# A softmax over a vocabulary: VectorE's and ScalarE's programs as loops, with six pieces a tile for five

## Chip, cores and metric

One core of a Trainium2 chip. The metric is the device time of one execution in microseconds (us). Before the change, three runs gave 2490.64, 2491.82 and 2493.5 us, median 2491.82.

## The reference

```python
batch, seq, vocab = 16, 256, 32768          # logits, float32; temperature 1.0
scaled = logits / temperature
scaled = scaled - scaled.max(axis=-1, keepdims=True)
exp_scaled = np.exp(scaled)
return exp_scaled / exp_scaled.sum(axis=-1, keepdims=True)
```

It is a softmax of 4096 rows of 32768 floats: 537 MB are read and 537 MB written.

## The kernel before, in words

A row is cut into two halves of 16384 floats, which lie on neighbouring partitions. So there are 8192 half rows, and 64 tiles of 128 partitions x 16384 floats (8 MB each). Three places in the on-chip memory (`xs`) hold one tile each; tile g stands in place g mod 3 and is computed in place.

Within a tile the work goes by five pieces of 4096, 4096, 4096, 2560 and 1536 columns (L11):

- VectorE takes each piece's maximum, negated (L146). ScalarE then takes the exponential with this maximum as bias, in place, and adds the piece up as it goes (L159). Every piece so has its own maximum and its own sum.
- When the last exponential is done, VectorE swaps maxima and sums with the neighbouring partition (a stream shuffle, L173), takes the least negated maximum of the row (L177), ScalarE turns the differences into ten correction factors (`ee`, L184), VectorE multiplies and adds (L190), inverts (L202) and makes one factor a piece (L209).
- Then the pieces are scaled in place: two of them on ScalarE (L216, those of `_ON_ACT`, 4096 and 2560 columns), three on VectorE (L219).

All this is written out for 64 tiles, one after the other: the program of each engine is straight, with one running semaphore for each engine (`Stream`, L17) and two sets of small tiles (`t`, `ee`, `junk`, `row`) used in turn. VectorE's own order is maxima, totals, scalings of one tile, and then the maxima of the next; it does not start a tile before the one before it is scaled.

SP issues all transfers on one queue, in an order written out by hand (`transfers`, L63). In the middle of the run it is: load of tile i, as soon as tile i-3 has been stored; store of tile i-1, as soon as it is scaled; and so on. A load is issued at L242, a store at L265. The ends differ: tile 0 comes as a load of 15360 columns and sixteen narrow ones of 8 rows x 1024 columns (L253), tile 3 and the store of tile 0 come in halves, and the store of the last tile, 63, goes in four quarters of 4096 columns, each when its own columns are scaled. `loads` and `stores` (`Lanes`, L44) are semaphores that count sixteen for each transfer, one mark from each of the sixteen DMA engines.

Of the kernel before, what the change touches and what calls it, by code (L numbers as in the profile page):

```python
# [8 lines left out]
_W = 16384  # L9
_BUFS = 3  # L10
_PIECES = (4096, 4096, 4096, 2560, 1536)  # L11
_ON_ACT = (2, 3)
_LAST_STORE = 4096
_NARROW = 1024


class Stream:  # L17


    def __init__(self, nc, engine, name):  # L20
        self.engine = engine
        self.sem = nc.alloc_semaphore(name)
        self.count = 0
        self.seen = {}

    def wait(self, *tokens):
        need = {}
        for sem, value in tokens:
            key = id(sem)
            if value > max(self.seen.get(key, 0), need.get(key, (None, 0))[1]):  # L30
                need[key] = (sem, value)
        for key, (sem, value) in need.items():
            self.engine.wait_ge(sem, value)
            self.seen[key] = value

    def done(self, instruction):
        self.count += 1
        instruction.then_inc(self.sem, 1)
        return (self.sem, self.count)


class Lanes:


    def __init__(self, nc, name):
        self.nc = nc
        self.name = name
        self.sems = {}
        self.counts = {}

    def add(self, key, instruction):
        if key not in self.sems:
            self.sems[key] = self.nc.alloc_semaphore(f"{self.name}_{'_'.join(map(str, key))}")
            self.counts[key] = 0
        self.counts[key] += 16
        instruction.then_inc(self.sems[key], 16)
        return (self.sems[key], self.counts[key])

    def tokens(self):
        return [(self.sems[k], self.counts[k]) for k in self.sems]  # L60


def transfers(n):  # L63
    half = _W // 2
    whole = [(0, _W)]
    halves = [(0, half), (half, half)]
    quarters = [(s, _LAST_STORE) for s in range(0, _W, _LAST_STORE)]
    wide = [(0, _W - _NARROW)]
    plan = [("L", 0, wide), ("N", 0, [(_W - _NARROW, _NARROW)]), ("L", 1, whole), ("L", 2, whole)]
    plan += [("S", 0, halves), ("L", 3, halves), ("S", 1, whole), ("S", 2, whole)]  # L70
    for i in range(4, n - 2):
        plan += [("L", i, whole), ("S", i - 1, whole)]
    plan += [("L", n - 2, whole), ("L", n - 1, whole)]
    plan += [("S", n - 3, whole), ("S", n - 2, whole), ("S", n - 1, quarters)]
    return plan
# [3 lines left out]
def kernel(  # L79
# [20 lines left out]
    K = len(_PIECES)  # L100
    starts = [sum(_PIECES[:k]) for k in range(K)]
    assert sum(_PIECES) == _W
# [4 lines left out]
    T = [nc.alloc_sbuf_tensor(f"t{q}", [P, 4 * K], fp32) for q in range(2)]  # L107
    E = [nc.alloc_sbuf_tensor(f"ee{q}", [P, 2 * K], fp32) for q in range(2)]
    J = [nc.alloc_sbuf_tensor(f"junk{q}", [P, 2 * K], fp32) for q in range(2)]
    R = [nc.alloc_sbuf_tensor(f"row{q}", [P, 4], fp32) for q in range(2)]  # L110

    sp = Stream(nc, nc.sync, "sp")
    dve = Stream(nc, nc.vector, "dve")
    act = Stream(nc, nc.scalar, "act")
    loads = Lanes(nc, "ld")
    stores = Lanes(nc, "st")
    landed = {}
    stored = {}
    scaled = {}
    hist = {}  # L120

    def overlapping(parts, s, n):
        return [token for (a, m), token in parts.items() if a < s + n and s < a + m]

    class Tile:

        def __init__(self, g):
            self.g = g
            self.base = (g % _BUFS) * _W
            self.t, self.e, self.j, self.r = T[g % 2], E[g % 2], J[g % 2], R[g % 2]  # L130
            self.tv = self.t[:, 0 : 4 * K].rearrange("p (a b k) -> p a b k", a=2, b=2)
            self.sums = None
            scaled[g] = {}

        def piece(self, k):
            s = self.base + starts[k]
            return X[:, s : s + _PIECES[k]]

        def exponentials(self, k):
            t = self.t  # L140
            if k == 0 and self.g >= 2:
                dve.wait(*hist[self.g - 2])
            xs = self.piece(k)
            dve.wait(*overlapping(landed[self.g], starts[k], _PIECES[k]))
            m = dve.done(
                nc.vector.tensor_reduce(  # L146
                    out=t[:, k : k + 1], in_=xs, axis=mybir.AxisListType.X, op=A.max, negate=True
                )
            )
            if inv_t != 1.0:  # L150
                dve.wait(m)
                m = dve.done(
                    nc.vector.tensor_scalar_mul(
                        out=t[:, k : k + 1], in0=t[:, k : k + 1], scalar1=inv_t
                    )
                )
            act.wait(m)
            self.sums = act.done(
                nc.scalar.activation(  # L159
                    out=xs,  # L160
                    in_=xs,
                    func=Exp,
                    bias=t[:, k : k + 1],
                    scale=inv_t,
                    accum_out=t[:, K + k : K + k + 1],
                )
            )

        def totals(self):
            t, e, r, tv = self.t, self.e, self.r, self.tv  # L170
            dve.wait(self.sums)
            sh = dve.done(
                nc.vector.stream_shuffle(out=t[:, 2 * K : 4 * K], in_=t[:, 0 : 2 * K], mask=swap)  # L173
            )
            dve.wait(sh)
            mx = dve.done(
                nc.vector.tensor_reduce(  # L177
                    out=r[:, 0:1], in_=tv[:, :, 0, :], axis=mybir.AxisListType.XY, op=A.min
                )
            )  # L180
            act.wait(mx)
            ev = e[:, 0 : 2 * K].rearrange("p (a k) -> p a k", a=2)
            ee = act.done(
                nc.scalar.activation(  # L184
                    out=ev, in_=tv[:, :, 0, :], func=Exp, bias=r[:, 0:1], scale=-1.0
                )
            )
            dve.wait(ee)
            tr = dve.done(
                nc.vector.tensor_tensor_reduce(  # L190
                    out=self.j[:, 0 : 2 * K].rearrange("p (a k) -> p a k", a=2),
                    in0=ev,
                    in1=tv[:, :, 1, :],
                    scale=1.0,
                    scalar=0.0,
                    op0=A.mult,
                    op1=A.add,
                    accum_out=r[:, 1:2],
                )
            )  # L200
            dve.wait(tr)
            rc = dve.done(nc.vector.reciprocal(out=r[:, 2:3], in_=r[:, 1:2]))  # L202
            dve.wait(rc)
            hist[self.g] = (ee, tr)

        def scale(self):
            f = self.j
            w = dve.done(
                nc.vector.tensor_scalar_mul(out=f[:, 0:K], in0=self.e[:, 0:K], scalar1=self.r[:, 2:3])  # L209
            )  # L210
            act.wait(w)
            dve.wait(w)
            for k in range(K):
                xs = self.piece(k)
                if k in _ON_ACT:
                    token = act.done(nc.scalar.mul(out=xs, in_=xs, mul=f[:, k : k + 1]))  # L216
                else:
                    token = dve.done(
                        nc.vector.tensor_scalar_mul(out=xs, in0=xs, scalar1=f[:, k : k + 1])  # L219
                    )  # L220
                scaled[self.g][starts[k], _PIECES[k]] = token
            hist[self.g] += tuple(scaled[self.g].values())

    def compute(g):
        a = Tile(g)
        for k in range(K):
            a.exponentials(k)
        a.totals()
        a.scale()

    plan = transfers(G)
    for (what, g, parts), (what_next, _, _) in zip(plan, plan[1:] + [(None, None, None)]):
        base = (g % _BUFS) * _W
        rows = slice(g * P, (g + 1) * P)
        if what == "L":
            landed[g] = {}
            for k, (s, n) in enumerate(parts):
                if g >= _BUFS:
                    sp.wait(*overlapping(stored[g - _BUFS], s, n))
                landed[g][s, n] = loads.add(  # L240
                    (g % _BUFS, k),
                    nc.sync.dma_start(out=X[:, base + s : base + s + n], in_=x[rows, s : s + n]),  # L242
                )
# [59 lines left out]
```

## Time and profile before

| what | value |
|---|---|
| profiled execution | 2491.0 us |
| span of its trace | 2489.2 us |
| moved by DMA | 1073.89 MB, mean 431 GB/s over the span |
| DMA busy, by slices | 9 tenths or more in 39 of 40 slices, 8 in the last |
| VectorE: maxima (L146), 320 | 1117.3 us busy |
| VectorE: scalings (L219), 192 | 354.9 us busy |
| ScalarE: exponentials (L159), 320 | 965.9 us busy |
| ScalarE: scalings (L216), 128 | 385.9 us busy |
| VectorE waits for loads (L146) | 681.3 us in 60 waits |
| VectorE waits for the last exponential (L173) | 221.4 us in 64 waits |
| load, issue to landing, median | 48.4 us |
| store, issue to landing, median | 29.5 us |

A tile's own chain on the engines, from the start of its first maximum to the end of its last scaling, is about 28 us (tile at 2370.60: last scaling ends at 2398.95). The tiles follow each other at 38.6 us in the middle of the run.

How to read the views: DVE is VectorE, ACT is ScalarE, SP the engine that issues transfers. The busy share of an engine is a mean over the span. A DMA share of 1.00 means that all sixteen DMA engines work; packets are counted where they start, so a short window can show more than 1. The queue called "instruction" carries the engines' own programs from memory. The trace also keeps each DMA packet's start, size and duration, and the moment of each completion mark; where the text speaks of those, they are read from these records. In the tables of windows "x" counts instructions.

### The profile page before, as it was taken

Reading aid. Unit: us, or ns where it says so; the run is one execution under the profiler, and the core shown is the slowest. Engines: PE = TensorE matmul, PEld = TensorE weight load, DVE = VectorE, ACT = ScalarE, POOL = GpSimd, SP = SyncE. Lnnn points to the kernel's source line nnn. Section 1 sums busy time; section 2 is a strip of 40 time slices with the busy share of each in tenths; the row PEclk is TensorE's granted clock in tenths of the full one; section 3 lists DMA queues with packets and bytes.
Section 4 is the critical chain, followed back from the end, with each engine's and each line's share of the span. In section 5 each row is a group of like instructions: output and inputs, shape, how many; then the busy total and the mean of one; then the engine's idle time right before and its main releaser. Section 6 shows DMA issues by size and latency. Waiting matters only on the chain.

```text
span 2489.2 us, 2061 instructions
## 1 busy us (share of the span) xinstructions
DVE 1529.5 (61%) x960; ACT 1390.4 (56%) x833; POOL 0.2 (0%) x4
## 2 busy tenths in 40 slices
DVE  5845665655656556565565665656656566565664
ACT  4744654646546455464554645646556465564655
POOL 0000000000000000000000000000000000000000
DMA  9999999999999999999999999999999999999998
GB/s 411 439 432 429 438 437 434 426 436 437 428 434 437 437 429 432 438 434 434 431 436 436 436 428 436 438 433 432 433 438 432 429 437 435 432 431 438 430 429 368
DMA packets 19425, 1073.89 MB, mean 431 GB/s; under 512 B 2256, under 2 KB 2256, under 8 KB 2384
## 3 DMA queue, kind: packets, MB, share of 16 engines
q1 hardware_dynamic: 19408, 1073.75, 99.8%
q14 instruction: 17, 0.14, 0.0%
HBM read 536.87 MB, written 536.87 MB: 431 GB/s over the span
## 4 chain that ended last, share of the span: by engine, by line
DMA 60%; DVE 19%; ACT 18%; another core or an unknown queue 1%; issue 0%; SPq 0%
DMA xs<-in_logits_dram 57%; DVE t L146 17%; ACT xs L159 10%; ACT xs L216 7%; DMA out_dram<-xs 3%; DVE xs L219 1%; ACT ee L184 0%; SPq L265 0%; DVE junk L209 0%; DVE row L202 0%; DVE row L177 0%; DVE t L173 0%; DVE junk L190 0%; DVE row L190 0%
## 5 line engine op out<-in xcount | busy, mean ns | idle before, releaser
L146 DVE TENSOR_REDUCE t<-xs 128x1 f32<-128x4096 f32 (+2 forms) x320 | 1117.3, 3558 | 681.3 <-DMA xs<-in_logits_dram 681.3
L159 ACT ACTIVATE xs<-xs,t 128x4096 f32<-128x4096 f32 (+2 forms) x320 | 965.9, 3019 | 1000.7 <-DVE t L146 1000.7
L216 ACT ACTIVATE xs<-xs,junk 128x4096 f32<-128x4096 f32 (+1 forms) x128 | 385.9, 3062 | 45.5 <-DVE junk L209 45.5
L219 DVE TENSOR_SCALAR xs<-xs,junk 128x4096 f32<-128x4096 f32 (+1 forms) x192 | 354.9, 1906 | 2.3
L173 DVE LOAD_MASK_SELECT t<-t x64 | 0.9, 14 | 221.4 <-ACT xs L159 221.4
L159 ACT ACTIVATION_READ_ACCUMULATOR xs<-xs,t 128x1 f32 x320 | 59.6, 186 | 0.0
L184 ACT ACTIVATE ee<-t,row 128x10 f32<-128x10 f32 x64 | 19.5, 305 | 27.9 <-DVE row L177 27.9
L190 DVE CUSTOM_DVE_ANT_1 junk<-ee,t 128x10 f32<-128x10 f32 x64 | 10.9, 170 | 23.8 <-ACT ee L184 23.8
L209 DVE TENSOR_SCALAR junk<-ee,row 128x5 f32<-128x5 f32 x64 | 14.8, 231 | 2.2
L202 DVE RECIPROCAL row<-row 128x1 f32<-128x1 f32 x64 | 10.5, 164 | 2.2
L177 DVE TENSOR_REDUCE row<-t 128x1 f32<-128x10 f32 x64 | 10.5, 164 | 2.2
L173 DVE STREAM_SHUFFLE t<-t 128x10 f32<-128x10 f32 x64 | 10.4, 162 | 0.0
L190 DVE DVE_READ_ACCUMULATOR2_ANT row<- 128x1 f32 x64 | 5.3, 83 | 0.0
L159 ACT ACT_TABLE_LOAD x1 | 1.3, 1283 | 0.9 <-SPq L105 0.9
L284 POOL MEMSET const-bfloat16-1.0<- 128x1 bf16 x1 | 0.1, 101 | 0.0
L284 POOL MEMSET const-uint8-127<- 128x1 uint8 x1 | 0.1, 101 | 0.0
L284 POOL MEMSET const-float32-0.0<- 128x1 f32 x1 | 0.1, 98 | 0.2 <-issue 0.2
L284 POOL MEMSET const-float32-1.0<- 128x1 f32 x1 | 0.1, 98 | 0.0
## 6 DMA issues: line engine op xcount, KB each, us to landing
out_dram<-xs SPq DMA_DIRECT2D x2, 4096.0 KB, 29.2
xs<-in_logits_dram SPq DMA_DIRECT2D x2, 4096.0 KB, 19.4
out_dram<-xs SPq DMA_DIRECT2D x4, 2048.0 KB, 16.5
xs<-in_logits_dram SPq DMA_DIRECT2D x1, 7680.0 KB, 20.7
xs<-in_logits_dram SPq DMA_DIRECT2D x62, 48.4
out_dram<-xs SPq DMA_DIRECT2D x62, 29.5
xs<-in_logits_dram SPq DMA_DIRECT2D x16, 32.0 KB
```

The lines of the kernel that those rows point to most:

```text
L146: nc.vector.tensor_reduce(out=t[:, k : k + 1], in_=xs, axis=mybir.AxisListType.X, op=A.max, negate=True)
L159: nc.scalar.activation(out=xs, in_=xs, func=Exp, bias=t[:, k : k + 1], scale=inv_t, accum_out=t[:, K + k : K + k + 1],)
L173: nc.vector.stream_shuffle(out=t[:, 2 * K : 4 * K], in_=t[:, 0 : 2 * K], mask=swap)
L177: nc.vector.tensor_reduce(out=r[:, 0:1], in_=tv[:, :, 0, :], axis=mybir.AxisListType.XY, op=A.min)
L184: nc.scalar.activation(out=ev, in_=tv[:, :, 0, :], func=Exp, bias=r[:, 0:1], scale=-1.0)
L190: nc.vector.tensor_tensor_reduce(out=self.j[:, 0 : 2 * K].rearrange("p (a k) -> p a k", a=2), in0=ev, in1=tv[:, :, 1, :], scale=1.0, scala ...
L202: rc = dve.done(nc.vector.reciprocal(out=r[:, 2:3], in_=r[:, 1:2]))
L209: nc.vector.tensor_scalar_mul(out=f[:, 0:K], in0=self.e[:, 0:K], scalar1=self.r[:, 2:3])
L216: token = act.done(nc.scalar.mul(out=xs, in_=xs, mul=f[:, k : k + 1]))
L219: nc.vector.tensor_scalar_mul(out=xs, in0=xs, scalar1=f[:, k : k + 1])
L284: nc = _bacc.Bacc("TRN2", target_bir_lowering=False, num_devices=1)
```

## The change

VectorE and ScalarE each get a program of their own: four tiles written out (`_HEAD`), then a loop of 20 turns (`engine.Fori`), each of three tiles. The running semaphores are replaced by one for each event and each place in the turn (`Signals`, `Place`): the loop waits for the same semaphores in each turn, with the turn's number (or sixteen times that for loads) as the value, taken from a register. VectorE makes the sixteenfold once a turn (`engine.snap`).

Six pieces of falling width replace the five; the last three are scaled by ScalarE (6720 columns, 6656 before). VectorE shuffles the maxima as soon as the last of them is taken and finds the row's maximum while ScalarE is still at its exponentials; the sums are shuffled on their own, later. Two `hold`s a tile wait and count a semaphore in an instruction of their own ahead of a shuffle. The small tiles have three sets in place of two. The transfers, their sizes and their order on SP are those of before; a store now waits for the last piece of VectorE and the last of ScalarE that it covers.

The core of the diff:

```diff
-_PIECES = (4096, 4096, 4096, 2560, 1536)
-_ON_ACT = (2, 3)
+_PIECES = (3584, 3200, 2880, 2560, 2240, 1920)
+_ON_ACT = (3, 4, 5)
+_HEAD = 4
...
+class Place:
+    def __init__(self, g, turn=None, turn16=None):
+        self.g = g
+        self.slot = g % _BUFS
+        if g == 0:
+            self.key, self.n, self.n16 = ("z",), 1, 16
+        else:
+            self.key = ((g - 1) % _BUFS,)
+            self.n = (g - 1) // _BUFS + 1 if turn is None else turn
+            self.n16 = 16 * ((g - 1) // _BUFS + 1) if turn16 is None else turn16
...
+        def wait(self, engine, *key):
+            engine.wait_ge(sig[(*key, *self.p.key)], self.p.n)
+        def hold(self, engine, *key):
+            self.wait(engine, *key)
+            engine.sem_inc(sig[("passed",)], 1)
+        def done(self, instruction, *key):
+            instruction.then_inc(sig[(*key, *self.p.key)], 1)
...
+            self.hold(v, "max", K - 1)
+            self.done(v.stream_shuffle(out=t[:, 2 * K : 3 * K], in_=t[:, 0:K], mask=swap), "sh")
+            self.wait(v, "sh")
+            self.done(v.tensor_reduce(out=r[:, 0:1], in_=tv[:, :, 0, :], ..., op=A.min), "mx")
+            self.hold(v, "sum", K - 1)
+            self.done(
+                v.stream_shuffle(out=t[:, 3 * K : 4 * K], in_=t[:, K : 2 * K], mask=swap), "shs"
+            )
...
+    for engine, part in ((nc.vector, Work.vector), (nc.scalar, Work.scalar)):
+        for g in range(_HEAD):
+            part(Work(Place(g)))
+        with engine.Fori(2, 2 + (G - _HEAD) // _BUFS) as turn:
+            turn16 = engine.snap(turn * 16) if engine is nc.vector else None
+            for j in range(_BUFS):
+                part(Work(Place(_HEAD + j, turn, turn16)))
```

`Work.vector` is the part of one tile on VectorE (maxima, shuffles, totals, its three scalings), `Work.scalar` that on ScalarE (six exponentials, the correction factors, its three scalings).

## The prediction

> **What bounds the kernel now.** I read the page first, its engine shares beside its DMA rows.
>
> ```profile
> DVE 1529.5 (61%) x960; ACT 1390.4 (56%) x833; POOL 0.2 (0%) x4
> ...
> DMA  9999999999999999999999999999999999999998
> ...
> q1 hardware_dynamic: 19408, 1073.75, 99.8%
> q14 instruction: 17, 0.14, 0.0%
> ```
>
> The engines are idle 40% of the time and the sixteen DMA engines almost never. The DMA records of the trace say how rigid that is: a 64 KB packet takes 2418 ns at the median, at the 5th and at the 75th percentile alike, so a whole-tile transfer, eight such packets on each DMA engine, takes 19.34 us, and a tile (a load and a store) 38.7 us. 64 tiles are 2476 us of the 2489.2. The bound is the bytes; the change moves none of them.
>
> Then the timeline, at one store and the next load, to see what cover the engines' work has.
>
> ```profile
> 454.13 5.55 DVE L219 TENSOR_SCALAR xs<-xs,junk 128x4096 f32<-128x4096 f32 x3
> 454.13 6.03 ACT L216 ACTIVATE xs<-xs,junk 128x4096 f32<-128x4096 f32 x2 [0.71 <-DVE junk L209]
> 460.24 0.33 SPq L265 DMA_DIRECT2D out_dram<-xs  x1
> ...
> 472.27 4.42 DVE L146 TENSOR_REDUCE t<-xs 128x1 f32<-128x4096 f32 x1 [12.59 <-DMA xs<-in_logits_dram]
> ```
>
> The store joins the queue 12.0 us before the load ahead of it has landed (10.2 us at most other tiles, 228.37 against 238.56). So the engines may become 10 us slower or any amount faster per tile, and the DMA engines do not notice. The chain of waits puts 17% on VectorE and 18% on ScalarE; that is time beside running transfers.
>
> What is left is 13 us at both ends. I read the tail by windows (columns: length, busy of DVE, ACT, POOL, clock, DMA share, GB/s).
>
> ```profile
> 2459.00:2462.40 3.40, 3.33 (x4) 3.00 (x1) 0.00 (x0) 1.00 0.36 154
> 2462.40:2480.00 17.60, 2.55 (x2) 3.03 (x2) 0.00 (x0) 1.00 1.00 426
> ...
> 2482.40:2485.20 2.80, 0.00 (x0) 0.00 (x0) 0.00 (x0) 1.00 0.17 70
> 2485.20:2489.20 4.00, 0.00 (x0) 0.00 (x0) 0.00 (x0) 1.00 0.04 16
> ```
>
> Two facts: from 2459.0 to 2462.4 about half of the DMA engines have nothing, as the last tile is not yet scaled; and from 2482.4 on only a few work (0.17 of sixteen is three, 0.04 is one). **The end is set by one late DMA engine.** Which one, and since when, the completion marks tell: each transfer counts its semaphore up sixteen times, once per DMA engine. Lag behind the early engines, us, of the last three:
>
> ```
> transfer landed   102.7  451.1  762.1  782.4 1110.8 1131.0 1769.3 1789.6 2468.6 2488.0
> last                2.6    3.2    4.5    5.5    5.4    6.4    7.2    8.2    8.8    5.3
> second              2.5    3.2    4.4    4.4    4.8    4.9    5.8    5.8    6.4    3.0
> third               2.5    3.0    3.8    3.8    4.5    4.5    5.7    5.7    6.3    2.8
> ```
>
> Eight engines start 2.4 us late (the narrow first loads lie on them). The last engine then jumps at 119, 458, 769, 1118, 1445, 1776, 2103 and 2436 us, by 0.7 to 1.1 each, 7.0 in all, 0.88 on average. At each of those moments the trace has one 8 KB packet of the instruction queue (309 ns), and a data packet beside it that takes 460 to 860 ns over its 2418. These eight are about 327 us apart, 8.5 tiles, and VectorE executes 960/64 = 15 instructions a tile, so 127 in between: 128 instructions of 64 bytes are the 8 KB. They are VectorE's program being fetched. Seven more, 10 tiles apart at ScalarE's 833/64 = 13, fall on a second engine (0.3 to 0.7 each, 3.4 in all); two (737, 2365) are SP's, on a third, which also drifts by some 0.03 us a transfer from a cause I do not see. The last table column shrinks because the early engines waited 3.2 us in the hole at 2459.
>
> **The change, part by part.**
>
> *Loops.* VectorE's program shrinks from some 960 instructions to a head of four tiles and a body of three. By the built order a tile is 16 shown rows, two mask loads and three instructions that only wait or count, 21; the body with its branch about 66, the head about 88. ScalarE: 16 a tile, body 50, head 68. Before, VectorE's first fetch comes 51 to 56 instructions in (tile 3, at 119 us), the next 128 later. The loop stands at about 90 to 156, between two fetch points (56 and 184); ScalarE's, at 70 to 120, between about 44 and 172. If a turn stays inside what has been fetched, VectorE's eight become one and ScalarE's seven one; SP's two stay. VectorE's DMA engine then loses 7 x 0.88 = 6.2 of its 8.8 us of lag, ScalarE's 6 x 0.49 = 2.9 of 6.3 or so. SP's keeps 6.3, and is now last. The end comes where the second and third column end: 5.3 - 2.9 = **2.4 us earlier**. This is the whole gain that I count.
>
> [...]
>
> *The branch and the register.* Twenty branches, a register step and a multiply on VectorE have no row. Bounds: nothing, and 10 us a turn, the idle time ahead of L146; I take nothing, as any of it lies in that idle time (10.8 us at the load's wait). Without the cover each turn's cost would count twenty times.
>
> *Six pieces.* From the rows by form, a maximum costs 1.043 ns an element and 0.14 us, an exponential 0.84 ns and 0.27. The six maxima take 17.52 us against 17.46; the last exponential ends at 19.6 against 20.9, as the last piece's maximum is no longer ahead of ScalarE by a queue of work. *Maxima shuffled early:* shuffle, minimum and most of the `ee` step now stand beside the exponentials; the scaling starts at 20.6 against 22.3. ScalarE's three scalings take 2414 + 2149 + 1881 less two overlaps of 0.09 = 6.26 against 6.03. Tile: 26.9 against 28.35 us, 1.5 saved, all of it under cover: the store only waits longer in the queue. Costs if the cover were gone: it would be a gain of 64 x 1.5, so this part has no losing side. The three extra wait or count instructions a tile have no row; bounds are nothing and 0.2 us each (the shuffle's row is 0.16), under the same cover.
>
> *The hole at 2459.* Tiles 62 and 63 run back to back, so the first quarter is ready 3.5 us earlier by the two tiles' chains, less 1.5, since it now ends with the second of two DVE pieces: 1.9 earlier. The early engines' 3.2 us of idleness becomes 1.3. Worth nothing at the end: SP's and VectorE's engines were 6 and 9 us behind and never idle there. It would be worth something only if all lags were under 3.
>
> *Semaphores and buffers per place.* Three sets of small tiles for two, and waits on constants: queue order on SP is unchanged, transfers too. Its store now waits for two semaphores in place of one or two; both come before the same moment. Nothing.
>
> Sum on the profiled run: span 2489.2 - 2.4 = 2486.8; with the 1.8 us around the span (2491.0 - 2489.2), 2488.6. The median of the runs shown is 0.8 above the profiled run, so **2489.4**.
>
> **Rivals.** *A, the forecast:* fetches nearly gone, SP's engine ends last, 2489.4; 2487.5 to 2492 with the spread of the runs shown (2490.64 to 2493.5) laid around it. For it: the steps coincide with the fetches. Against it: the third engine's drift is unexplained.
>
> *B, the loop fetches anew each turn (slower).* If a taken branch makes VectorE's sequencer drop what it holds, each turn brings at least one 8 KB packet: 21 in place of 8 on the same DMA engine, 18.5 in place of 7.0 us, 2491.8 + 11.5 = 2503; two a turn give 2521. It decides from eight fetches on; from about 14 the loss passes 0.2%. [...] Against it: the body, 66 instructions, is half of one block, and no fetch point lies in it.
>
> [...] No run so far shows a loop.
>
> *C, SP's engine is no limit (faster).* If its drift goes with the work of the other two (their semaphore traffic), its lag falls under 3 too and the end is that of the thirteen: 5.3 earlier, 2486.5. For it: nothing but the unknown cause. *D, the fetches cost nothing.* If the data packets beside a fetch are slow for another reason, and the 309 ns are caught up elsewhere, the lags stay and the time is 2491.8. For it: slow packets also come in groups without a fetch (around 465 and 2420). Against it: seven of VectorE's eight fetches have a jump of the last column alone. [...]
>
> **How the numbers follow.** About 0.2%, 5 us, is what a measurement of this kernel can tell from no change. A 0.57, D 0.09, C 0.16, B 0.18. C lies just over the bound of faster, and a little of A's spread with it; B is slower. Faster 0.17, same 0.66, slower 0.17. The range holds A, D and C: 2485 to 2494. B is left out with its 0.18.
>
> **What would show it.** Right: the page's instruction queue falls from 17 to about 4 packets; the last transfer's marks spread over 3 us, not 5.4; DMA share stays 9 in all slices; DVE's wait for the load grows by 1.5 a tile; the first exponential starts at 3.9 us of a tile, not 4.45. Wrong: 25 packets or more in that queue with a last engine 15 us late (B); spread under 1 us (C); idle DMA engines in mid-run, or fetches gone and the same end (D).

## The result, and the profile after

Over 20 runs each, the changed kernel takes 2488.55 us (median; 2488.42 to 2488.80), the kernel before 2492.48 (2489.32 to 2493.89). The ratio is 0.9985, 95% interval 0.9979 to 0.9991: 3.9 us faster. The profiled execution takes 2488.64 us, its span 2486.8 us. Not only the median fell; the runs now lie within 0.4 us, where those of the kernel before lie within 4.6.

The page of the changed kernel, the rows that answer to those shown of before:

```profile
DVE 1543.8 (62%) x1152; ACT 1419.5 (57%) x1025; POOL 0.2 (0%) x4
...
DMA  9999999999999999999999999999999999999998
...
q1 hardware_dynamic: 19408, 1073.75, 99.7%
q14 instruction: 4, 0.03, 0.0%
```

More instructions are executed (six pieces), the data are the same, and the instruction queue has 4 packets where it had 17. In the trace's DMA records they come at 95, 98, 734 and 2363 us: one for VectorE, one for ScalarE, and SP's two. None comes from the loops.

A tile in the middle, from the timeline (start, duration, engine, operation):

```profile
439.61 2.96 ACT L264 ACTIVATE xs<-xs,t 128x3200 f32<-128x3200 f32 x1
...
453.00 6.27 ACT L285 ACTIVATE xs<-xs,junk 128x2560 f32<-128x2560 f32 x3 [0.87 <-DVE junk L248]
453.00 5.51 DVE L254 TENSOR_SCALAR xs<-xs,junk 128x3584 f32<-128x3584 f32 x3
459.34 0.33 SPq L165 DMA_DIRECT2D out_dram<-xs  x1
459.72 0.42 SPq L147 DMA_DIRECT2D xs<-in_logits_dram  x1
470.95 17.52 DVE L202 TENSOR_REDUCE t<-xs 128x1 f32<-128x3584 f32 x6 [12.44 <-DMA xs<-in_logits_dram]
```

The store is issued 11.6 us before the load ahead of it has landed, 10.2 us at most tiles before. The tail by windows (length, busy of DVE, ACT, POOL, clock, DMA share, GB/s), in nearly the stretches of before:

```profile
2456.00:2459.00 3.00, 3.00 (x3) 3.00 (x2) 0.00 (x0) 1.00 0.40 175
2459.00:2462.40 3.40, 1.35 (x1) 2.10 (x2) 0.00 (x0) 1.00 0.89 376
...
2480.00:2482.40 2.40, 0.00 (x0) 0.00 (x0) 0.00 (x0) 1.00 0.06 27
2482.40:2485.20 2.80, 0.00 (x0) 0.00 (x0) 0.00 (x0) 1.00 0.05 23
```

The hole before the last store has moved 3 us ahead. From 2480 on one DMA engine works alone (0.06 of sixteen is one). The completion marks say which, as before: lag behind the early engines, us.

```
transfer landed   103.8   722.3   742.3  2349.2  2369.3  2466.2  2485.6
last                3.7     4.0     4.7     8.2     8.9     9.3     6.0
second              3.1     3.8     3.8     3.9     4.0     3.9     0.6
third               2.6     3.2     3.2     3.2     3.3     3.2     0.2
```

The places change hands once: at 104 us VectorE's engine is last with 3.7 and ScalarE's second with 3.1, just after their one fetch, and they keep that within 0.2 to the end. SP's passes them by 700 us and is the last from there on, with a step at each of its fetches (734, 2363) and a drift between. It landed tile 62's store at 2466.1 us before (2459.7 and a lag of 6.4) and at 2466.2 now: nothing changed for it. VectorE's, which was 2.5 us later still, no longer sets the end, and the last mark moves from 2488.0 to 2485.6.

### The profile page after: what moved, and what is told of

It reads as the page before. It is cut to its first block, busy times and chain, and to the rows that moved or that the text cites. A ratio compares the mean times of both kernels' runs of the same rounds, so it can differ in the third digit from the quotient of the medians.

```text
span 2486.8 us, 2759 instructions
## 1 busy us (share of the span) xinstructions
DVE 1543.8 (62%) x1152; ACT 1419.5 (57%) x1025; POOL 0.2 (0%) x4
## 4 chain that ended last, share of the span: by engine, by line
DMA 52%; ACT 29%; DVE 10%; another core or an unknown queue 6%; issue 2%; SPq 0%; DVEq 0%; ACTq 0%
DMA xs<-in_logits_dram 49%; ACT xs L264 24%; DVE t L202 6%; ACT xs L285 5%; DMA out_dram<-xs 3%; DVE xs L254 3%; DVE junk L248 0%; SPq L165 0%; DVE t L227 0%; DVE row L245 0%; DVE junk L232 0%; DVEq L187 0%; DVE row L232 0%; ACTq L298 0%
## 5 line engine op out<-in xcount | busy, mean ns | idle before, releaser
L202 DVE TENSOR_REDUCE t<-xs 128x1 f32<-128x3584 f32 (+5 forms) x384 | 1121.2, 2989 | 783.0 <-DMA xs<-in_logits_dram 783.0
L264 ACT ACTIVATE xs<-xs,t 128x3584 f32<-128x3584 f32 (+5 forms) x384 | 984.9, 2565 | 985.4 <-DVE t L202 983.9
L285 ACT ACTIVATE xs<-xs,junk 128x2560 f32<-128x2560 f32 (+2 forms) x192 | 401.1, 2152 | 55.3 <-DVE junk L248 55.3
L254 DVE TENSOR_SCALAR xs<-xs,junk 128x3584 f32<-128x3584 f32 (+2 forms) x192 | 352.8, 1893 | 2.3
L264 ACT ACTIVATION_READ_ACCUMULATOR xs<-xs,t 128x1 f32 x384 | 71.5, 186 | 0.0
L277 ACT ACTIVATE ee<-t,row 128x12 f32<-128x12 f32 x64 | 18.4, 288 | 0.0
L248 DVE TENSOR_SCALAR junk<-ee,row 128x6 f32<-128x6 f32 x64 | 14.8, 231 | 2.2
L232 DVE CUSTOM_DVE_ANT_1 junk<-ee,t 128x12 f32<-128x12 f32 x64 | 11.0, 172 | 2.2
L220 DVE TENSOR_REDUCE row<-t 128x1 f32<-128x12 f32 x64 | 10.6, 166 | 2.2
L217 DVE STREAM_SHUFFLE t<-t 128x6 f32<-128x6 f32 x64 | 10.6, 166 | 0.6
L227 DVE STREAM_SHUFFLE t<-t 128x6 f32<-128x6 f32 x64 | 10.5, 163 | 0.6
## 6 DMA issues: line engine op xcount, KB each, us to landing
xs<-in_logits_dram SPq DMA_DIRECT2D x1, 7680.0 KB, 20.7
```

What stands on the lines that cost most here:

```text
L202: m = v.tensor_reduce(out=t[:, k : k + 1], in_=self.piece(k), axis=mybir.AxisListType.X, op=A.max, negate=True,)
L217: self.done(v.stream_shuffle(out=t[:, 2 * K : 3 * K], in_=t[:, 0:K], mask=swap), "sh")
L220: v.tensor_reduce(out=r[:, 0:1], in_=tv[:, :, 0, :], axis=mybir.AxisListType.XY, op=A.min),
L227: v.stream_shuffle(out=t[:, 3 * K : 4 * K], in_=t[:, K : 2 * K], mask=swap), "shs"
L232: v.tensor_tensor_reduce(out=f[:, 0 : 2 * K].rearrange("p (a k) -> p a k", a=2), in0=self.ev, in1=tv[:, :, 1, :], scale=1.0, scalar=0.0, o ...
L248: v.tensor_scalar_mul(out=f[:, 0:K], in0=e[:, 0:K], scalar1=r[:, 2:3]), "f"
```

## Experiments

The theory, F: a fetch of instructions delays one DMA engine (0.88 us a fetch on VectorE's in the trace of before); a transfer counts as landed when all sixteen marks are in, and the last one sets the end. The rivals: P, the pieces and the shorter chain gained it; H, the scaling of the last tile sets the end. All runs differ from the changed kernel by the edit shown; in longer edits `...` stands for what is left out. They were timed in three groups, and each ratio is to the kernel before as timed in the same group. That kernel's median was 2492.06, 2493.15 and 2492.35 us in the three, so medians of different groups can differ by a microsecond for that reason alone. "Remaining" below is the time from a store's issue to the first completion mark of the load in flight: the work that the early DMA engines still have.

**The loops alone, undone.**

```diff
-        with engine.Fori(2, 2 + (G - _HEAD) // _BUFS) as turn:
-            turn16 = engine.snap(turn * 16) if engine is nc.vector else None
-            for j in range(_BUFS):
-                part(Work(Place(_HEAD + j, turn, turn16)))
+        for g in range(_HEAD, G):
+            part(Work(Place(g)))
```

> The changed kernel with its two loops written out: same pieces, same semaphores, same order, 60 tiles more in each program. Theory F (what the change gained is the fetches): 21 instructions a tile on VectorE are 10 to 11 fetches of 8 KB in place of 1, 16 a tile on ScalarE are 8, with SP's two about 21 packets in the instruction queue. VectorE's DMA engine then lags 2.5 + 10 x 0.88 = 11.3 us behind the early ones, more than SP's (9.3), and the end comes 2.0 us later than with loops: about 2490.6, and the runs differ among themselves by more than the 0.4 us of the changed kernel. Rival P (the pieces and the shorter chain gained it, the fetches are beside it): 2488.6, as with loops.

Measured: 2496.64 us (2496.20 to 2498.02), ratio to the kernel before 1.0020 (1.0011 to 1.0029). The page:

```profile
q14 instruction: 21, 0.17, 0.0%
```

21 packets, as expected, and VectorE's engine is last: from 100 us on, its time from landing to landing is longer by 0.95 to 0.97 us in nine of the ten transfers with a fetch (0.80 in the last). P falls: with all its pieces and its shorter chain the program without loops is slower than the old one. The expected size was too small, 2.0 us where 8.1 are lost. With these prices the fetches alone put VectorE's engine 13.4 us behind where the early engines of the changed kernel are (its lag there, 3.9, and ten more fetches), 4.1 behind SP's. The rest, 3.7 us, comes from 1700 us on, in groups of 8 to 19 slow packets a tile that no fetch goes with. They slow the last engine by 0.1 to 0.4 us at most tiles (0.8 at one), and the early ones more.

**The pieces alone, undone.**

```diff
-_PIECES = (3584, 3200, 2880, 2560, 2240, 1920)
-_ON_ACT = (3, 4, 5)
+_PIECES = (4096, 4096, 4096, 2560, 1536)
+_ON_ACT = (2, 3)
```

> The changed kernel with the five old pieces (4096, 4096, 4096, 2560, 1536; two of them scaled by ScalarE), loops kept. Theory F: 4 packets in the instruction queue, SP's DMA engine last by 9 us, 2488.6 as with six pieces, though each tile's chain is 1 to 1.5 us longer. Rival P: the chain matters, so the time goes back towards the kernel before, 2491 to 2492.

Measured: 2487.79 us (2487.44 to 2488.90), ratio to before 0.9984 (0.9975 to 0.9993), 4 packets in the queue. The loops keep all the gain without the six pieces, so P falls from this side too. Whether the six cost something is open: the median is 0.8 us lower with five, but the two kernels were timed in different groups and their ratios to the kernel before, 0.9984 and 0.9985, do not separate them. In the profiled runs SP's engine is 8.1 us behind at the end, not 9.3. Why its drift should depend on the pieces, no run shows.

**A loop of 516 instructions a turn.**

```diff
+            for _ in range(150 if self.p.g >= _HEAD else 0):
+                v.sem_inc(sig[("padding",)], 1)
             for k in range(K):
```

> The changed kernel with 150 instructions more a tile in VectorE's loop, each of which only counts a semaphore, ahead of the tile's first maximum, where VectorE waits for the load anyway. A turn has 516 instructions (33 KB) in place of 66. Theory F: if the sequencer can't hold them, it fetches at least 516/128 = 4 packets a turn, 80 in the run, all on VectorE's DMA engine: 80 x 0.88 = 70 us more there, of which 5 are free until it passes SP's engine, so about 2550; if it can, 4 packets and 2488.6. Rival P: no change by fetches however many they are; at most the time of the added instructions, which have 12 us a tile of idle VectorE to lie in.

Measured: 2596.38 us (2595.82 to 2596.70), ratio 1.0417 (1.0402 to 1.0432).

```profile
q14 instruction: 122, 1.00, 0.1%
```

118 packets more, six a turn. VectorE's DMA engine had 5.4 us to spare before it would pass SP's; 107.7 us longer a span and those 5.4, over 118, are 0.96 us a fetch: the same price as above. The landings of the last engine say so directly: a transfer with no fetch beside it follows the one before after 19.3 us, one with two fetches after 21.3. The number of packets a turn was underestimated (six, not four), not the price. The DMA engine pays. VectorE stops at the branch as well (`DVE t L204 <- issue: 313.9, 20, 16.1` in its waits, added instructions included): in 19 of the turns its first maximum starts 1.8 us after the load has landed. The rest of that wait is time in which it would have waited for the load, and the 1.8 us stay under the store's cover (11.7 us at the store of 1162.64).

**Where the loop stops fitting:** 246 instructions a turn.

```diff
+            for _ in range(60 if self.p.g >= _HEAD else 0):
+                v.sem_inc(sig[("padding",)], 1)
```

> The changed kernel with 60 added counting instructions a tile in VectorE's loop, 246 a turn in place of 66 (516 with 150). It asks where the loop stops fitting. 246 instructions are two blocks of 8 KB at most three. Theory F: if no block is dropped, 4 to 6 packets in the instruction queue and 2488.6 to 2490; if blocks are fetched each turn, at least 40 packets, 0.9 us each on VectorE's DMA engine, of which 5 us are free: 2520 or more.

Measured: 2488.55 us in the one profiled run, 6 packets (at 96, 98, 188, 262, 736 and 2363 us: the two new ones are the longer program, fetched once). So a turn of 246 is not fetched again, and one of 516 is; where between them the limit lies is not measured.

**The late engine alone, relieved.** Three kernels move bytes between DMA engines. First, the last 1024 columns of tile 0 in one transfer:

```diff
-            if g == 0 and j == 1:
-                for q in range(0, P, 32):
-                    for r in range(4):
...
+            sig.dma(key, nc.sync.dma_start(out=X[:, where], in_=x[rows, s : s + n]))
```

> The changed kernel with the last 1024 columns of tile 0 loaded by one transfer of 128 rows in place of sixteen of 8 rows. Those sixteen lie on eight of the DMA engines (2.4 us more for them, nothing for the others); now all sixteen get half of that. Theory F, in its part that one late DMA engine (SP's, one of those eight) sets the end: it has 1.2 us less to move, so the end comes 1.2 us earlier, 2487.4. Rival H (the end is set by the last tile's scaling and the hole before its store): unchanged, 2488.6.

Measured: nine of twelve runs at 2486.74 to 2488.52, median 2487.46, as F expects; but three at 2503 to 2506, and over all of them the ratio to before is 0.9994 (0.9979 to 1.0009). The profiled run is one of the three (2505.77 us), and in it slow packets come at every tile from 155 us on. What sets off such a run is not shown, and this start is not alone in it: one of 25 runs of the kernel before took 2503.99 us in a later group, and one of twelve of a run below 2507.16. For F this run is weak.

Then four rows a transfer:

```diff
-                for q in range(0, P, 32):
-                    for r in range(4):
...
-                                out=X[q + r : q + 32 : 4, where],
...
+                for q in range(0, P, 4):
...
+                            out=X[q : q + 4, where],
...
```

> The changed kernel with the last 1024 columns of tile 0 loaded by 32 transfers of four rows in place of sixteen of eight. Those of eight rows lie on eight DMA engines; these should lie on four. Theory F, in its part that SP's DMA engine (one of the eight) sets the end: if it is not one of the four, it has 64 KB less to move, 2.4 us, and the time is 2486.1, with 12 early engines and four 4.8 us late; if it is one of the four, it has 64 KB more, and the time is 2491.0. Rival H (the last tile's scaling sets the end): 2488.6 in both cases.

Measured: 2488.69 us (2487.84 to 2489.96), ratio to before 0.9977 (0.9967 to 0.9986): neither of F's two numbers, and the one that H gave. The marks show why. SP's engine is not among the four late ones, and lands tile 62's store 2.2 us earlier than in the changed kernel (2464.0 against 2466.2). But VectorE's is among them and lands it at 2466.2, where SP's did. All engines lost some 2.4 us at the start besides: beside the narrow packets, the others' 64 KB packets take up to 2.2 us longer (4634 ns in place of 2418), which I had not counted. It is a miss in time, and by its time this run cannot tell F from H; only the marks say that another late engine took the place of SP's.

The third keeps the transfers of four rows, has half of the narrow columns, and issues them behind tile 1's load.

```diff
-_NARROW = 1024
+_NARROW = 512
...
-    plan = [("L", 0), ("L", 1), ("L", 2), ("S", 0), ("L", 3), ("S", 1), ("S", 2)]
+    plan = [("L", 0), ("L", 1), ("N", 0), ("L", 2), ("S", 0), ("L", 3), ("S", 1), ("S", 2)]
...
+                for q in range(0, P, 4):
...
```

> The changed kernel with 512 columns of tile 0 (not 1024) in 32 transfers of four rows, issued behind the load of tile 1, so that tile 1's load does not wait 20 us for their issue as it did in the run with 1024. Four DMA engines, VectorE's and ScalarE's among them, get 64 KB, the other twelve, SP's among them, none. Against the changed kernel SP's engine has 48 KB less to move (496 KB of tile 0 in place of 544), 1.8 us, and VectorE's 16 KB more (560). Theory F (one late DMA engine sets the end): 1.8 us earlier if SP's engine keeps its drift (2486.8), up to 4 us earlier (2484.6) if it drifts as little as in the run with 1024 columns, where VectorE's comes last at 4.4 us behind. Rival H (the last tile's scaling sets the end): 2488.6.

Measured: 2485.97 us (2485.61 to 2486.10), ratio to before 0.9973 (0.9962 to 0.9984), within the expected 2484.6 to 2486.8. The time is F's and not H's. But the last tile is scaled earlier here too (its first store is issued at 2456.1 us, at 2458.8 in the changed kernel), as its load comes earlier, so this run alone does not refute H. The times of issue do. In the changed kernel the four last stores are all issued by 2462.0 us, and SP's engine lands the store ahead of them only at 2466.2; its four quarters then follow in 19.4 us without a gap. With five pieces alone the last of these stores is issued 0.6 us later than in the changed kernel, and the end comes 1.1 us earlier (2484.5 against 2485.6).

The same with the five old pieces:

```diff
+_PIECES = (4096, 4096, 4096, 2560, 1536)
+_ON_ACT = (2, 3)
...
+_NARROW = 512
...
```

> The same with the five old pieces, where SP's engine drifted 1.2 us less and the time was 0.8 us less. Theory F: 0 to 1 us below the run with six pieces, 2484 to 2486.5. Rival H: 2488, as with five pieces alone.

Measured: 2485.38 us (2484.79 to 2485.92), ratio 0.9970 (0.9959 to 0.9982): the fastest of all, 7.0 us below the kernel before in its group, with the loops, the five old pieces and this start. And with 1024 columns again (`_NARROW = 1024`, five pieces, behind tile 1's load):

> The same with five pieces and 1024 columns. Four DMA engines get 128 KB of them, VectorE's among these, and start 4.8 us behind the others. Theory F: VectorE's engine is last, with 6.8 us behind twelve engines that start where the early ones of the changed kernel start: 2.5 us below the changed kernel, 2486.1, and more than the run with 512 columns. Rival H: 2488.

Measured: 2488.60 us at the median (eleven runs at 2487.70 to 2489.76, one at 2507.16), ratio to before 0.9989 (0.9975 to 1.0003), not 2486.1. As with four rows above, the narrow packets slow the others' at 40 to 50 us, here by up to 2.7 us each. With 512 columns the slowest such packet took 1.3 to 1.4 us over, and in the changed kernel, at 21 to 24 us, 0.9. H gave 2488 here as well, but its last store is issued 2.1 us later than in the changed kernel and the end comes only 0.2 us later (2485.8).

**What the groups of slow packets come from.**

```diff
-_ON_ACT = (3, 4, 5)
+_ON_ACT = (2, 3, 4, 5)
```

> The changed kernel with four pieces scaled by ScalarE in place of three: its scalings take 8.9 us in place of 6.3, so each store is issued 2.7 us later, 9.0 us ahead of the landing of the load before it in place of 11.7. No fetch is added. Theory M (the groups of slow packets that the kernel before shows from 1830 us on, and the written-out one from 1625 us on, begin where the early DMA engines have less than one packet, 2.4 us, left when the store is issued): groups of slow packets begin where SP's engine lags more than 6.6 us, at about 1550 us, once a tile; the written-out kernel had 0.2 us a tile on its last engine from them, so 24 tiles give some 4 us, 2492. Rival G (the groups come from the fetches): no groups, 2488.6.

Measured: 2490.98 us (2488.93 to 2496.82), ratio to before 0.9994 (0.9984 to 1.0004). All ten runs are above the slowest of the changed kernel (2488.80), which was timed with another group of runs; the run with 246 instructions a turn, timed with these, took 2488.55. The loss is smaller than the 4 us expected. The store is later, as two lines of its timeline show (9.0 us ahead of the landing):

```profile
422.94 0.33 SPq L165 DMA_DIRECT2D out_dram<-xs  x1
...
431.96 3.89 DVE L202 TENSOR_REDUCE t<-xs 128x1 f32<-128x3584 f32 x1 [14.06 <-DMA xs<-in_logits_dram]
```

4 packets in the instruction queue, and the groups are there: first at 1350 us, at nearly every tile from 1780 on. Theory G falls. Sorted by what the early engines have remaining at a store's issue (tiles from 150 to 2400 us; 64 KB packets over 2500 ns, from one store's issue to the next; 2418 is usual):

```
kernel               remaining under 2.5 us            2.5 us or more
before               16 tiles, 6.3 slow a tile         42 tiles, 1.0 a tile (19 of the 40 in one tile)
written out          21 tiles, 13.2                    36 tiles, 0.3
late store           22 tiles, 6.7                     35 tiles, 1.0
516 a turn           52 tiles, 20.8                    3 tiles, 2.3
one transfer         32 tiles, 12.3                    25 tiles, 3.6
changed              none                              58 tiles, 0.03
five pieces          none                              58 tiles, 0.03
512 columns, six     none                              58 tiles, 0.4
512 columns, five    none                              58 tiles, 0.6
```

Four pieces on ScalarE, straight code or the old kernel: the large groups come where about one packet, 2.4 us, or less is left. The limit is not sharp: the late store has 3 to 8 slow packets in each of five tiles with 2.5 to 2.8 us left, and a few tiles under 2.5 us have none. Nor is this the only source of slow packets: the kernel before has 19 in one tile with 7.1 us left, and the kernel with one transfer, in its profiled run of 2505.77 us, up to 12 a tile with 2.6 to 8.8 us left. Lag (8.8 us in the kernel before) and lateness of the store (9.0 us ahead of the landing in the late store, 11.6 in the changed kernel) work together. That the spread of the runs comes from these groups is argued, not shown: the late store's spread is 7.9 us with no fetch added, and the changed kernel, the one with five pieces and the two fastest, which have no such groups, lie within 0.4 to 1.5. Against it stands the one run in twelve at 2507.16 with five pieces and 1024 columns, whose profiled run, a usual one, has at most two slow packets a tile.

**What SP's engine drifts by.**

```diff
-    if g == 3:
-        return [(0, _W // 2), (_W // 2, _W // 2)]
-    return [(0, _W)]
+    return [(0, _W // 2), (_W // 2, _W // 2)]
...
```

That is for the loads of all tiles but tile 0; the stores of all tiles but the last have the same edit.

> The changed kernel with every load and store in two halves, twice the transfers and nearly twice SP's instructions for the same bytes. It asks what SP's DMA engine falls behind by (0.042 us for each whole-tile transfer, 5.3 us in the run, beside 0.75 for each of its two fetches). If by what SP does: the drift doubles, 5.3 us more, and one or two fetches of SP are added, about 2495. If by the bytes or by the engine itself: the drift stays, 2488.6 to 2490.

Measured: 2498.77 us (2497.97 to 2499.29), ratio to before 1.0020 (1.0010 to 1.0029), more than both. A 32 KB packet takes 1213 ns at the median, two of them 2426: 8 ns more than one of 64 KB, on all engines, 8 us over some thousand pairs. SP's engine drifts 7.5 us in place of 5.3 (12.4 behind at the end, less 2.6 at the start and three fetches of 0.75), neither doubled nor the same. In the run with four rows and 1024 columns it drifted about 3. The cause of the drift stays open.

## Why the prediction was right, step by step

**The bound, and the late engine.** Right. The predicted span was 2486.8 us and the measured one is 2486.8; the predicted time of a profiled run was 2488.6 and it is 2488.64; 2489.4 was the forecast for a median, 2488.55 is measured. The end did go to where the second and third column ended.

**The loops between two fetch points.** Right: one fetch each, and 4 packets in all. The trace of the changed kernel has 21 VectorE instructions a tile, as counted. A turn of 246 was fetched once (6 packets in the run, after 262 us SP's two alone), and one of 516 brought 118 packets more, six a turn; the limit lies between the two, and where and by what it is set, no run shows. The packets are 8 KB each, one for about every 127 of VectorE's instructions in the kernel before. What rival B describes does come with a turn of 516 (118 fetches, 108 us); the loop of 66 stays clear of it, and that of 246 too, so a branch alone does not bring it. VectorE's one branch of before brings no packet either: it stands at 0.77 us, and from there to 104 us the instruction queue has none.

**The branch and the register, costed at nothing.** Right. In the trace of the changed kernel a turn's branch takes VectorE 0.06 us, the register step 0.04 and the multiply 0.05, and in all 20 turns they lie within the time of its scalings. A wait or count instruction takes 0.02 us, where the bound was 0.2.

**The price of a fetch, 0.88 us.** Near for VectorE: 0.96 in most single steps of the written-out kernel, 0.96 on the mean of 118, 0.8 in some. Too small for ScalarE: 0.49 was worked with, and in the written-out kernel, up to 1660 us, the step is about 0.66 (0.31 for the packet, 0.34 to 0.36 in the data packet beside it). So both engines gained more than forecast: VectorE's lands tile 62's store 7.8 us earlier than before (6.2 forecast), ScalarE's 6.0 (2.9 forecast), the slow groups' part included. Neither sets the end any more, so the forecast time did not suffer. For VectorE's eight fetches of before, the data packet that starts as the fetch ends takes 0.23 to 0.64 us over its 2418 ns, not 0.46 to 0.86.

**SP's engine keeps its lag of 6.3.** Its place on the clock, yes; its lag, no: 9.3. The early engines are 2.9 us earlier; before, they lose that in steps at the tiles with slow groups (0.65 us at 460, 0.8 by 2250 and again by 2420), and these groups are gone. So the sign given for the last transfer, marks spread over 3 us, failed: they spread over 6.1. The other signs came: 4 packets, a DMA share of 9 in all slices but the last, 1.7 us more a tile in VectorE's wait for the load (783.0 us in 60 waits, 681.3 before; 1.5 was forecast). Rival C, that its drift would go too, is refuted.

**The hole of 3.2 becomes 1.3.** Wrong: an early engine's gap there is 3.1 us. The first store of tile 63 is issued 3.0 us earlier (2458.75 against 2461.78): 1.7 of it come from the two tiles' chains, near the 1.9 worked out, and 1.3 from tile 62's load, which landed earlier. But the early engines arrive 2.9 us earlier as well. It was rightly costed at nothing.

**The tile's chain.** Predicted 26.9 us, scaling from 20.6, first exponential at 3.9; measured 27.0 (470.95 to 497.92), 20.7 and 3.9.

**"The engines may become 10 us slower per tile, and the DMA engines do not notice."** This is the step that failed. The 10 us are the cover of the last DMA engine. The early ones were up to 8.8 us ahead of it, and had as little as 1.4 us left; in the 16 tiles with under 2.5 us left, about one packet, 6.3 packets a tile are slow, in the 42 others 1.0. The late-store run, 2.7 us later a tile, is 2.4 us slower than the changed kernel and spreads over 8. So the shorter chain was not worth nothing by its kind: it keeps 1.5 us more of that cover. With loops and five pieces the cover holds as well (2.65 us at the least, 2.55 with six), which is why the pieces themselves bring nothing.

**3.9 us in the median where 2.4 were worked out.** The 2.4 are the two profiled executions (2491.0 and 2488.64). The other 1.5 are the median of before above its own profiled run. The forecast took 0.8 for that from three runs, and carried it over to the changed kernel, which has no such spread. So of the 3.9 us only the 2.4 were worked out beforehand.

## To carry to other kernels

When the DMA engines are busy all along, look at the sixteen completion marks of single transfers: the last engine's lag, 9.3 us here, is time that no engine's busy share shows. Of these 9.3 us on SP's engine, the narrow first loads have 2.6 and its two fetches 1.5; the rest is the drift whose cause stays open. A fetch of 0.31 us cost its engine two to three times that (0.66 to 0.96). Loops of 66 and of 246 instructions a turn did not fetch again, one of 516 did, six packets a turn; count a loop's instructions, and look at the instruction queue's packets. And measure cover for the earliest DMA engine, not for the last, and keep more than one packet remaining: here slow groups came at up to 2.8 us, with a packet of 2.4.

## What was not expected of the hardware

- A fetch of 8 KB took 0.309 us, and the data packet that starts as it ends took longer as well (by 0.23 to 0.64 us for VectorE's eight of before). By the landings it cost its DMA engine 0.96 us for VectorE's and about 0.66 for ScalarE's (written-out kernel), 0.73 for SP's (changed kernel).
- In the changed kernel, from 150 to 2400 us, 96 of 100 packets of 64 KB take 2418 ns to the nanosecond. Where the early engines have about one packet or less left when the store is issued, 6 to 21 packets a tile, on the mean of a run, take 0.1 to 1 us more.
- 128 narrow packets of 4 KB on four engines slowed 64 KB packets on the others by up to 2.7 us. Transfers of four rows do lie on four engines: the marks show four late by 5.1 to 5.5 us.
- Now and then a run is 11 to 19 us longer than the median of its kernel: three in twelve with the last columns of tile 0 in one transfer, one in twelve with five pieces and 1024 columns in transfers of four rows, one in 25 of the kernel before. What sets it off stays open.
